# A decoder trunk's hidden steps re-paced: modulation steps at least four granules apart, the second norm's constants behind the output projection, seven fill steps in the norm gap

## The chip, the cores and the metric

One core of a Trainium2 chip runs the whole program. The metric is the device time in microseconds of one execution, lower being better. The kernel before took 2029.11 us in the median of three runs (2023.68 to 2029.93). In the profile PE is the matrix engine (PEld its weight loads), DVE, ACT and POOL are the vector, scalar and general engines, and SP issues most transfers.

## What is computed

One layer of a decoder trunk in float32, for 256 prompt rows and 8 sample rows (264 columns in all, `NT`), width D = 2048. Cut to what matters here:

```python
mod = silu(c) @ w_ada + b_ada                      # 2048 x 12288, nine rows of c
sh1, sc1, gt1, sh2, sc2, gt2 = split(mod, 6)
h = rmsnorm(x, g_pre_mix) * (1 + sc1) + sh1
z = h @ w_in                                       # u, v, q, f, i, ..., three gates
...                                                # branch A: spatial gating
...                                                # branches B, C: gated linear recurrences
merged = sum(sigmoid(gate_n) * (branch_n @ w_branch[n]) for n in range(3))
x = x + gt1 * rmsnorm(merged @ w_out, g_post_mix)
h2 = rmsnorm(x, g_pre_mlp) * (1 + sc2) + sh2
x = x + gt2 * rmsnorm(square(relu(h2 @ w_up)) @ w_down, g_post_mlp)
```

The recurrences also return their final states, and for the eight samples every state (128 x 128 or 128 x 256 a head) is read, updated and written.

## The kernel before

**The large products.** Activations lie transposed, features on partitions, 264 columns wide. Weights stream in as a list of blocks (`Stream`). A block of 512 KB (tile `raw`) is split by ACT (line 111, tile `whi`) and DVE (line 108, tile `wlo`) into a high and a low part, and `granule` issues its 24 matmuls: two output blocks, four blocks of the inner dimension, three products (lines 542 to 544). A granule is the unit in which everything else is paced; 578 are issued, and I count them from the program's start. Blocks are loaded five granules ahead and split two ahead. After each granule `linear` calls `background()`, which counts `now[0]` up by one.

**The hidden work.** Three queues are pumped there. `bg` runs the mixers (transposes, gates, decays, the levels of the recurrence, the outputs), `bs` runs the samples' states, and `ba` runs the modulation: `ada_round(r)` computes one sixth of `mod` in 16 steps. A step is four products with weights of 32 columns and 512 moving columns each (line 290, tile `ada`; eight records in the trace) on two tiles `araw` of 512 KB each. There are two such tiles (`ADA_RAW`), and a step's last statement asks SP for the next two, which can be loaded only once the step's matmuls have read the old ones. SP issues in order, `raw` and `araw` in one line.

**Slots.** A level's matmuls (line 562) and a sample's (line 569) are not issued where they arise but collected in `levels` and `samples` and issued in a `slot()`, at the earliest `AGE` = 2 granules later. A slot opens when the modulation has 0.9 steps owing (0.27 come in per granule), or when something waits and a modulation step may go along (`ba.owed >= 0.0`; a step lowers it by one), or when something has waited three granules. So every level or sample that becomes due while `ba.owed` is not negative takes a modulation step with it, wherever the last one was.

**Samples.** For each of eight samples and each group of heads, `samples_r` has POOL load the state (`st`, line 950) and the value row spread over the partitions (`vbc`, line 955), ACT scales the state (line 975), DVE adds the outer product (line 977), POOL writes it back (line 978), and PE reads it (line 569) into `os`. `finish(i)` is called when a branch needs group i: it drains what is left of the mixer and of the group's samples, and transposes `os` on PE (line 1178).

**Who sets the order.** In the mixer stage PE and POOL keep the order of the program (`manual_schedule`, left at line 1280), while DVE, ACT and SP are ordered by the scheduler of the language. Behind line 1280 the scheduler orders PE as well.

**Behind the mixers.** `ba.drain()` finishes the modulation; `G1`, `A2` and `B2` are made of it; the output projection runs 32 granules (`gated_rows` takes each result), and meanwhile 12 tiles for the last modulation round are loaded into free blocks (`pre`, six steps' worth). Then PE has no projection until the two norms are through: `norms()` (lines 1316, 1318), the residual (line 1342), `norm_rows` (squares on line 211, the samples' sum on line 200, a reciprocal root of eleven small DVE instructions), the scaling (lines 1351, 1352), transposes on PE (line 227), and `modulate` on DVE and ACT (lines 358, 360, then 111 and 108). This is the norm gap. Into it go fill steps of round 5: `fill.pump(5.0)` takes the loading step and four steps, `fill.pump(9.0)` nine more, 13 steps in all. What is left goes on in the MLP at 0.2 a granule, one step in six granules.

Of the kernel before, what the change touches and what calls it, by code (L numbers as in the profile page):

```python
# [11 lines left out]
ALU = mybir.AluOpType  # L12
# [3 lines left out]
P = 128  # L16
D = 2048
KT = D // P
# [3 lines left out]
NC = 1 + NS  # L22
# [23 lines left out]
LOAD_AHEAD = 5  # L46
SPLIT_AHEAD = 2
N_BRANCH = 3
FILL = (5.0, 9.0)
READY = object()  # L50
SLOT_LATE = 0.9
SLOT_WAIT = 3
# [1 line left out]
LEVELS_HELD = 3  # L54
FETCHED = 3
AGE = 2


@with_exitstack
def hybrid_step_kernel(  # L60
# [37 lines left out]
    def const(shape, name, dt=F32):  # L98
        return cp.tile(shape, dt, tag=name, name=name)
# [432 lines left out]
    def granule(w, k0, n, c0, width, accs, xh, xl, k, first, last):  # L532
# [11 lines left out]
                    T.matmul(o, b, xh(k + j), start=False, stop=last and j == n - 1)  # L544
        stream[0].ahead()

    levels, samples = [], []

    def slot():

        lv = [x for x in levels if x[0] + AGE <= now[0]][:2]
        sv = [x for x in samples if x[0] + AGE <= now[0]]
        del levels[:len(lv)]
        del samples[:len(sv)]
        if lv:
            pl = sm([P, 2, 8, 32])
            for i, (_, lhs, rhs, _) in enumerate(lv):
                for h in range(4):
                    for hf in range(2):
                        for b in range(4):  # L560
                            t0 = hf * P + b * 32
                            T.matmul(pl[32 * b:32 * b + 32, i, 2 * h + hf, :], lhs[:, h, t0:t0 + 32], rhs[:, h, t0:t0 + 32], start=True, stop=True)  # L562
        if sv:
            G, qm, os_ = sv[0][1]
            nh = 512 // G.dv
            po = sm([P, G.dv])
            for h in range(4):
                for i, (_, _, b, sts) in enumerate(sv):
                    T.matmul(po[32 * h:32 * h + 32, :], qm[:, h, b, :], sts[h // nh][:, h % nh, :], start=i == 0, stop=i == len(sv) - 1)
        if ba.g and ba.owed >= 0.0:  # L570
            ba.step()
        for i, (_, _, _, put) in enumerate(lv):
            put(pl[:, i])
        if sv:
            if sv[0][2] == 0:
                V.tensor_copy(os_, po)
            else:
                add(os_, os_, po)

    def background():  # L580

        now[0] += 1
        bg.pump(rate[0])
        bs.pump(rate[1])
        ba.owed = min(ba.owed + rate[2], SLOT_LATE) if ba.g else 0.0
        wait = max(now[0] + 1 - AGE - min([x[0] for x in levels + samples] + [now[0]]), 0)
        if ba.owed >= SLOT_LATE or wait and (ba.g and ba.owed >= 0.0 or wait >= SLOT_WAIT):
            slot()

    def new_acc():  # L590
# [2 lines left out]
    def linear(w, k0, nk, c0, width, xh, xl):  # L593

        acc = new_acc()
        kc = min(nk, 1024 // width)
        for kb in range(0, nk, kc):
            granule(w, k0, kc, c0, width, [acc], xh, xl, kb, kb == 0, kb + kc == nk)
            background()
        return acc[:, 0:width // P, 0:NT]  # L600
# [392 lines left out]
    def mixer_r(G):  # L993
# [101 lines left out]
        S.activation(ft.unsqueeze(2), c[:, :, NP - 1:NP], AF.Exp)  # L1095
        yield
        mul(kd, kd, k[:, :, 0:NP])
        yield
        yield READY
        attx = blk([P, 4, P])  # L1100
        ps = sm([P, 4, P])
# [170 lines left out]
    order.__exit__(None, None, None)  # L1272


    ba.drain()
    G1 = const([P, KT, NC], "G1")
    mul(G1, mod[:, 2 * KT:3 * KT, :], gpostT.unsqueeze(2).to_broadcast([P, KT, NC]))
    A2 = const([P, KT, NC], "A2")
    V.scalar_tensor_tensor(A2, mod[:, 4 * KT:5 * KT, :], 1.0, gpre2T.unsqueeze(2).to_broadcast([P, KT, NC]), ALU.add, ALU.mult)
    B2 = mod[:, 3 * KT:4 * KT, :]  # L1280

    x1 = [[blk([P, 1024]) for _ in range(2)] for _ in range(2)]
    for t in range(2):
        for hf in range(2):
# [5 lines left out]
    def gated_rows(m, src, Gv, rows):  # L1290

        k = 2 * m
        sq = tmp([P, 2, NT], "vt")
        S.activation(sq, src, AF.Square)
        g = tmp([P, 2, NP], "gt")
        S.activation(g[:, 0, :], src[:, 0, 0:NP], AF.Copy, scale=Gv[:, k, 0:1])
        V.tensor_scalar(g[:, 1, :], src[:, 1, 0:NP], Gv[:, k + 1, 0:1], None, ALU.mult)
        pt = to_tokens(g)
        mul(gs[:, k:k + 2, :], src[:, :, NP:NT], Gv[:, k:k + 2, 1:NC])
        c0 = (m % 4) * CW  # L1300
        S.copy(rows[0][m // 4][:, c0:c0 + CW].rearrange("p (m f) -> p m f", m=2), pt[:, 0])
# [24 lines left out]
    for m in range(8):  # L1326
        if m in PRE_AT:
            n = N_PRE // len(PRE_AT)
            for k in range(n * PRE_AT.index(m), n * PRE_AT.index(m) + n):
                w = blk([P, 1024])  # L1330
                nc.sync.dma_start(w, w_ada[0, k // 2 * P:(k // 2 + 1) * P, 5 * D + k % 2 * 1024:5 * D + (k % 2 + 1) * 1024])
                pre.append(w)
        gated_rows(m, linear(w_out[0], 0, KT, m * CW, CW, mH, mL), G1, og)
    fill = Queue()
    fill.g.append(ada_round(5, pre))
    r1, r1s = norms()
# [131 lines left out]
```

## Time and profile before

| | |
|---|---|
| median of three runs | 2029.11 us |
| the profiled execution's own time | 2031.4 us |
| its span, first to last instruction | 2029.6 us |
| busy: PE, DVE, ACT, POOL | 1946.7, 1191.6, 998.4, 85.5 us |
| matmuls of the projections, lines 542 to 544 | 3 x 4624 records |
| records of modulation steps, line 290 | 464 (8 a step; some records are missing) |
| granted PE clock, mean | 0.982 |

The span begins at the first instruction and ends at the last. A row of a timeline gives the start, the duration, the engine, the line and operation, the tile written and the tiles read, and in brackets how long the engine had been idle and who released it. Rows of matmuls overlap, so the distance from one start to the next tells what a matmul costs. Times are us from the span's start: the mixers with their recurrences lie between about 404 and 966 us, the third branch until 1088, the output projection until 1215, the norm gap and the first MLP granules until 1276.

### The profile page before, as it was taken

The numbers are of one execution on the slowest core, as the hardware profiler recorded it, in microseconds if no ns is written. First come the engines' busy times: TensorE is split into PE (matmuls) and PEld (weight loads), VectorE is DVE, ScalarE is ACT, GpSimd is POOL, SyncE is SP. The second block draws the span as 40 slices with busy tenths as digits, with TensorE's granted clock in tenths as the row PEclk, the third lists the DMA queues.
The fourth block names the chain that finished last, engine by engine and source line by source line (L and its number), as shares of the span: only waits on it lengthen the run. The fifth ranks groups of instructions, "written<-read, shape, count | busy, mean of one in ns | idle before, by whom it ended". The sixth has DMA issues, their size and how long they took to land.

```text
span 2029.6 us, 42046 instructions
## 1 busy us (share of the span) xinstructions
PE 1946.7 (96%) x16972; PEld 1823.7 (90%) x16972; DVE 1191.6 (59%) x2094; ACT 998.4 (49%) x1773; POOL 85.5 (4%) x128
## 2 busy tenths in 40 slices
PE   6999999989979999999999998999999999999997
PEld 4889999878968888978999994899999999999997
DVE  3566667665656576455655556454555555555565
ACT  5444354655745564544444544455444444454543
POOL 1000000102101001120000000000000000000000
PEclk8999999999989999999999998999999999999998
DMA  9797797778578787788876865655555656556552
GB/s 303 276 344 253 230 304 222 224 224 233 170 227 230 227 239 228 218 256 277 282 247 196 269 199 176 210 183 179 182 182 179 185 178 183 181 180 183 179 177 95
DMA packets 341267, 442.05 MB, mean 218 GB/s; under 512 B 14930, under 2 KB 285008, under 8 KB 341072
## 3 DMA queue, kind: packets, MB, share of 16 engines
q1 hardware_dynamic: 330880, 409.19, 63.5%
q0 software_dynamic: 9120, 28.91, 5.5%
q8 instruction: 133, 2.18, 0.4%
q10 hardware_dynamic: 1072, 1.25, 0.2%
q14 instruction: 62, 0.51, 0.1%
HBM read 427.60 MB, written 11.70 MB: 216 GB/s over the span
## 4 chain that ended last, share of the span: by engine, by line
PE 85%; DMA 9%; DVE 2%; issue 1%; ACT 1%; SPq 0%; POOL 0%; DVEq 0%; ACTq 0%; POOLq 0%
PE mm L542 26%; PE mm L543 25%; PE mm L544 25%; DMA araw<-in_w_ada_dram 4%; PE ada L290 4%; DMA vbc<-vs_d 2%; PE ada L260 1%; DMA b<-in_w_ada_dram 1%; DVE wlo L108 1%; PE sm L703 1%; ACT whi L111 1%; DMA raw<-in_w_in_dram 1%; DMA st<-in_state_gla_dram 0%; DMA b<-in_x_prompt_dram 0%; PE sm L562 0%
## 5 line engine op out<-in xcount | busy, mean ns | idle before, releaser
L542 PE MATMUL mm<-b,whi 128*128 128x264 f32 x4624 | 1328.7, 287 | 7.3 <-DVE b L105 3.4
L543 PE MATMUL mm<-b,whi 128*128 128x264 f32 x4624 | 1320.5, 286 | 0.2 <-DVE b L108 0.2
L544 PE MATMUL mm<-b,wlo 128*128 128x264 f32 x4624 | 1315.8, 285 | 0.3 <-DVE wlo L108 0.2
L108 DVE TENSOR_TENSOR wlo<-raw,whi 128x512 fp32r<-128x512 f32 x1136 | 778.0, 690 | 628.1 <-ACT whi L111 625.7
L111 ACT CAST whi<-raw 128x512 fp32r<-128x512 f32 x1136 | 696.8, 618 | 811.3 <-PE mm L543 719.9
L542 PEld LDWEIGHTS mm<-b,whi 128*128 128x128 f32 x4624 | 873.9, 189 | 65.9 <-issue 29.7
L543 PEld LDWEIGHTS mm<-b,whi 128*128 128x128 f32 x4624 | 873.5, 189 | 5.6 <-issue 5.0
L544 PEld LDWEIGHTS mm<-b,wlo 128*128 128x128 f32 x4624 | 873.5, 189 | 0.7 <-DVE wlo L108 0.7
L105 DVE TENSOR_TENSOR b<-b,mm 128x528 f32<-128x528 f32 x136 | 95.6, 704 | 44.9 <-PE mm L544 44.9
L290 PE MATMUL ada<-araw,cT 128*32 128x512 f32 x464 | 89.3, 650 | 30.7 <-DMA araw<-in_w_ada_dram 30.6
L977 DVE SCALAR_TENSOR_TENSOR st<-vbc,b,st 128x128 f32<-128x128 f32 (+1 forms) x96 | 33.7, 393 | 72.4 <-DMA vbc<-vs_d 71.8
L975 ACT ACTIVATE st<-st,fs 128x128 f32<-128x128 f32 (+1 forms) x96 | 36.5, 429 | 55.6 <-DMA st<-in_state_gla_dram 28.4
L290 PEld LDWEIGHTS ada<-araw,cT 128*32 128x32 f32 x464 | 13.3, 111 | 51.3 <-DMA araw<-in_w_ada_dram 44.0
L260 PE MATMUL ada<-b,cT 128*32 128x256 f32 (+1 forms) x640 | 36.6, 362 | 10.8 <-DMA b<-in_w_ada_dram 10.4
L260 PEld LDWEIGHTS ada<-b,cT 128*32 128x32 f32 x640 | 18.0, 115 | 24.6 <-DMA b<-in_w_ada_dram 8.8
L102 DVE TENSOR_TENSOR b<-b,b 128x512 f32<-128x512 f32 (+1 forms) x47 | 34.2, 744 | 2.5 <-ACT b L1040 1.3
L978 POOL DMA_DIRECT2D out_dram<-st x32 | 23.5, 735 | 136.5 <-DVE st L977 91.0
L108 DVE TENSOR_TENSOR b<-gt,b 128x528 fp32r<-128x528 f32 x32 | 22.7, 708 | 3.3
L955 POOL DMA_DIRECT2D vbc<-vs_d x32 | 24.1, 754 | 1.8 <-DMA vs_d<-sqs 1.3
L111 ACT CAST whi<-araw 128x512 fp32r<-128x512 f32 x20 | 12.4, 621 | 21.6 <-PE mm L543 19.8
L108 DVE TENSOR_TENSOR b<-b 128x1024 f32<-128x1024 f32 (+1 forms) x21 | 22.4, 1069 | 1.0 <-PE sm L562 1.0
L102 DVE TENSOR_TENSOR gt<-vt 128x528 f32<-128x528 f32 x32 | 22.4, 700 | 0.0
(285 smaller groups left out, 812.8 us busy)
## 6 DMA issues: line engine op xcount, KB each, us to landing
raw<-in_w_in_dram SPq DMA_DIRECT2D x232, 512.0 KB, 4.8
raw<-in_w_mlp_up_dram SPq DMA_DIRECT2D x128, 512.0 KB, 3.9
raw<-in_w_mlp_down_dram SPq DMA_DIRECT2D x128, 512.0 KB, 3.6
araw<-in_w_ada_dram SPq DMA_DIRECT2D x116, 512.0 KB, 5.4
b<-in_w_ada_dram SPq DMA_DIRECT2D x60, 512.0 KB, 7.1
raw<-in_w_branch_dram SPq DMA_DIRECT2D x48, 512.0 KB, 4.5
raw<-in_w_out_dram SPq DMA_DIRECT2D x32, 512.0 KB, 3.7
b<-in_w_ada_dram SPq DMA_DIRECT2D x32, 256.0 KB, 6.4
```

Source lines behind the costliest of these rows:

```text
L102: V.tensor_tensor(o, a, b, op=ALU.mult)
L105: V.tensor_tensor(o, a, b, op=ALU.add)
L108: V.tensor_tensor(o, a, b, op=ALU.subtract)
L111: S.copy(hi, src)
L260: T.matmul(acc[32 * j:32 * j + 32, 0:n], cT[:, k, :], w[:, n * j:n * j + n], start=k == 0, stop=k == KT - 1)
L290: T.matmul(acc[32 * j:32 * j + 32, :], cT[:, k, :], ws[j // 2][:, j % 2 * 512:j % 2 * 512 + 512], start=k == 0, stop=k == KT - 1)
L542: T.matmul(o, a, xh(k + j), start=first and j == 0, stop=False)
L543: T.matmul(o, a, xl(k + j), start=False, stop=False)
L544: T.matmul(o, b, xh(k + j), start=False, stop=last and j == n - 1)
L955: nc.gpsimd.dma_start(v, vs_d[G.i, h * nj:h * nj + 4, b, :].partition_broadcast(P))
L975: S.activation(st[:, i, :], st[:, i, :], AF.Copy, scale=fs[:, h0 + i, b:b + 1])
L977: V.scalar_tensor_tensor(st[:, i, :], v[:, i, :], k[:, h0 + i, NP + b:NP + b + 1], st[:, i, :], ALU.mult, ALU.add)
```

## The change

Modulation gets a rule of its own, `ada_due()`: a step is taken only if at least four granules (`ADA_GAP`) have gone by since the last one was taken in a slot. A slot opens when a step is due and owing or something waits, or when something has waited three granules, so levels and samples may now be issued in a slot without a step. `ba.drain()`, `A2` and `B2` move behind the output projection. `FILL` goes from (5, 9) to (4, 4): the loading step and three steps, then four more, seven in all. In `mixer_r` the wait of a mixer ahead of its cross attention is written as two `READY` (each lets a granule go by and costs the queue nothing) in place of a plain `yield` (which costs it one) and one `READY`.

```diff
-FILL = (5.0, 9.0)
+FILL = (4.0, 4.0)
+ADA_GAP = 4
...
+    ada_at = [0]
+    def ada_due():
+        return ba.g and ba.owed >= 0.0 and now[0] >= ada_at[0] + ADA_GAP
...
-        if ba.g and ba.owed >= 0.0:
+        if ada_due():
+            ada_at[0] = now[0]
             ba.step()
...
-        if ba.owed >= SLOT_LATE or wait and (ba.g and ba.owed >= 0.0 or wait >= SLOT_WAIT):
+        if ada_due() and (ba.owed >= SLOT_LATE or wait) or wait >= SLOT_WAIT:
             slot()
...
         mul(kd, kd, k[:, :, 0:NP])
-        yield
+        yield READY
         yield READY
         attx = blk([P, 4, P])
...
-    ba.drain()
     G1 = const([P, KT, NC], "G1")
     mul(G1, mod[:, 2 * KT:3 * KT, :], gpostT.unsqueeze(2).to_broadcast([P, KT, NC]))
-    A2 = const([P, KT, NC], "A2")
-    V.scalar_tensor_tensor(A2, mod[:, 4 * KT:5 * KT, :], 1.0, gpre2T..., ALU.add, ALU.mult)
-    B2 = mod[:, 3 * KT:4 * KT, :]
...
         gated_rows(m, linear(w_out[0], 0, KT, m * CW, CW, mH, mL), G1, og)
+    ba.drain()
+    A2 = const([P, KT, NC], "A2")
+    V.scalar_tensor_tensor(A2, mod[:, 4 * KT:5 * KT, :], 1.0, gpre2T..., ALU.add, ALU.mult)
+    B2 = mod[:, 3 * KT:4 * KT, :]
```

Lines of the changed kernel are one to eight higher than before up to `mixer_r` and its like (290 is 291, 569 is 576, 1103 is 1111).

**The loads of modulation tiles on SP**, in the third recurrence (granules 184 to 200): each `raw` is one granule's block, each pair of `araw` belongs to the step that is taken next. Before:

```order
L283 DMA araw_8956<-in_w_ada_dram 128x1024
L283 DMA araw_8958<-in_w_ada_dram 128x1024
L502 DMA raw_8992<-in_w_in_dram 128x4x256
L502 DMA raw_9027<-in_w_in_dram 128x4x256
L502 DMA raw_9076<-in_w_branch_dram 128x4x256
L502 DMA raw_9114<-in_w_branch_dram 128x4x256
L283 DMA araw_9126<-in_w_ada_dram 128x1024
L283 DMA araw_9128<-in_w_ada_dram 128x1024
L502 DMA raw_9165<-in_w_in_dram 128x4x256
L283 DMA araw_9206<-in_w_ada_dram 128x1024
L283 DMA araw_9208<-in_w_ada_dram 128x1024
```

After:

```order
L284 DMA araw_9178<-in_w_ada_dram 128x1024
L284 DMA araw_9180<-in_w_ada_dram 128x1024
L503 DMA raw_9255<-in_w_in_dram 128x4x256
L503 DMA raw_9293<-in_w_in_dram 128x4x256
L503 DMA raw_9339<-in_w_in_dram 128x4x256
L503 DMA raw_9455<-in_w_branch_dram 128x4x256
L284 DMA araw_9414<-in_w_ada_dram 128x1024
L284 DMA araw_9416<-in_w_ada_dram 128x1024
L503 DMA raw_9496<-in_w_branch_dram 128x4x256
L503 DMA raw_9539<-in_w_in_dram 128x4x256
L503 DMA raw_9573<-in_w_in_dram 128x4x256
L503 DMA raw_9688<-in_w_in_dram 128x4x256
```

Before, the steps here are taken at granules 180, 184, 185, 190 and 192, so that a step follows its predecessor after four, one, five and two granules; now they are taken at 180, 184, 188, 192, 196 and so on. In the whole recurrence stage no step is nearer than four granules to the one before it, where before ten are. The last step of the mixers is taken at granule 284 instead of 272, and nothing is left for the drain behind the output projection.

**The cross attention's operand on DVE**, in the first recurrence (granules 124 to 128). Row L102 (L103) with `b_167` is the product `kd` that PE's lines 1103 (1111) read; `st<-vbc` are sample updates, each waiting for a `vbc` transfer. Before:

```order
L105 TENSOR_TENSOR os_923_5346<-os_923_5346,sm_5961 128x128
L108 TENSOR_TENSOR wlo_5996<-raw_5853,whi_5995 128x512
L977 SCALAR_TENSOR_TENSOR st_5957<-vbc_6069,b_4767,st_5957 128x128 x4
L108 TENSOR_TENSOR wlo_6000<-raw_5853,whi_5999 128x512
L977 SCALAR_TENSOR_TENSOR st_6067<-vbc_6215,b_4767,st_6067 128x128 x3
L102 TENSOR_TENSOR b_6016<-b_6016,b_167 128x512
L977 SCALAR_TENSOR_TENSOR st_6067<-vbc_6215,b_4767,st_6067 128x128
```

After:

```order
L109 TENSOR_TENSOR wlo_5990<-raw_5845,whi_5989 128x512
L103 TENSOR_TENSOR b_6006<-b_6006,b_167 128x512
L109 TENSOR_TENSOR wlo_6047<-raw_5919,whi_6046 128x512
L106 TENSOR_TENSOR os_921_5371<-os_921_5371,sm_6057 128x128
L109 TENSOR_TENSOR wlo_6051<-raw_5919,whi_6050 128x512
L109 TENSOR_TENSOR wlo_6095<-raw_5955,whi_6094 128x512
L985 SCALAR_TENSOR_TENSOR st_5957<-vbc_6106,b_4767,st_5957 128x128 x4
```

The product now stands ahead of the last two sample updates instead of behind one and three quarters of them; the granule at which PE reads it, 126, is the same.

**PE in the norm gap**, among the transposes of the normed rows (`sm`, line 227 or 228) and the modulation steps. Before, the second transposed tile is begun when a step's first half cuts in:

```order
L227 MATMUL sm_15066<-cst,b_15050 128x128
L227 MATMUL sm_15066<-cst,b_15052 128x128
L227 MATMUL sm_15078<-cst,b_15050 128x128
L290 MATMUL ada_14925<-araw_15006,cT 32x512 x2
L227 MATMUL sm_15078<-cst,b_15052 128x128
```

After, three transposed tiles (12 rows) run in a line before the first such row:

```order
L228 MATMUL sm_15035<-cst,b_14995 128x128
L228 MATMUL sm_15035<-cst,b_14997 128x128
L291 MATMUL ada_14918<-araw_15300,cT 32x512
L228 MATMUL sm_15047<-cst,b_14995 128x128
L228 MATMUL sm_15047<-cst,b_14997 128x128
```

Although seven steps are asked for in the gap, the scheduler has put two more and a quarter of a third early, ahead of or among the first projection's matmuls (before, seven steps stand behind the six of `pre`, most of them in halves, the last nearly six granules into the projections). In the MLP there are then a step's rest and six whole steps (granules 339 to 375) instead of two (333 and 339).

**PE at `finish(2)`**, told in words: before, the third group's last sample is read at granule 235 and `os` is transposed at 242; now the last sample's matmuls (line 576) stand at 242 directly ahead of the two transposes (line 1186), since its slot comes later and `finish` drains it.

More of the change, by code (lines that the diff above doesn't have):

```diff
@@ L1272, in hybrid_step_kernel @@
     order.__exit__(None, None, None)
-    ba.drain()
     G1 = const([P, KT, NC], "G1")
     mul(G1, mod[:, 2 * KT:3 * KT, :], gpostT.unsqueeze(2).to_broadcast([P, KT, NC]))
-    A2 = const([P, KT, NC], "A2")
-    V.scalar_tensor_tensor(A2, mod[:, 4 * KT:5 * KT, :], 1.0, gpre2T.unsqueeze(2).to_broadcast([P, KT, NC]), ALU.add, ALU.mult)
-    B2 = mod[:, 3 * KT:4 * KT, :]
     x1 = [[blk([P, 1024]) for _ in range(2)] for _ in range(2)]
@@ L1333, in hybrid_step_kernel @@
         gated_rows(m, linear(w_out[0], 0, KT, m * CW, CW, mH, mL), G1, og)
+    ba.drain()
+    A2 = const([P, KT, NC], "A2")
+    V.scalar_tensor_tensor(A2, mod[:, 4 * KT:5 * KT, :], 1.0, gpre2T.unsqueeze(2).to_broadcast([P, KT, NC]), ALU.add, ALU.mult)
+    B2 = mod[:, 3 * KT:4 * KT, :]
     fill = Queue()
```

## The prediction

> **What bounds the kernel.** I read the page first: its busy times, the chain of work that ended last, the costliest groups.
>
> ```profile
> PE 1946.7 (96%) x16972; PEld 1823.7 (90%) x16972; DVE 1191.6 (59%) x2094; ACT 998.4 (49%) x1773; POOL 85.5 (4%) x128
> PE 85%; DMA 9%; DVE 2%; issue 1%; ACT 1%; SPq 0%; POOL 0%; DVEq 0%; ACTq 0%; POOLq 0%
> 1345.00:2007.00 662.00, 662.00 (x5447) 661.03 (x5446) 385.58 (x590) 317.65 (x527) 0.00 (x0) 1.00 0.58 177
> ```
>
> PE is the bound. The third line, a window deep in the MLP, gives its pace: 662 us over 5447 rows, 0.1215 us a matmul, 2.9 us a granule of 24. The change removes no matmul, so only what stands between them can move: DMA has 9% of the chain. Next the waits of the stretch with the recurrences (404 to 966 us; waited for: total, times, longest), and windows of it and of the quiet stretch behind it (last columns: granted clock, DMA share, GB/s).
>
> ```profile
> PEld ada L290 <- DMA araw<-in_w_ada_dram: 35.1, 17, 7.6
> DVE st L977 <- DMA vbc<-vs_d: 71.8, 19, 6.3
> ACT st L975 <- DMA st<-in_state_gla_dram: 28.4, 12, 5.6
> ACT st L975 <- DMA st<-in_state_hgrn_dram: 27.1, 9, 5.3
> PEld sm L1103 <- DVE b L102: 5.0, 1, 5.0
> PEld sm L562 <- DVE b L102: 3.9, 1, 3.9
> ...
> 404.00:966.00 562.00, 527.34 (x5230) 473.48 (x5223) 332.96 (x622) 303.99 (x613) 68.31 (x95) 0.97 0.76 230
> 966.00:1088.00 122.00, 122.00 (x992) 114.14 (x991) 69.80 (x106) 56.40 (x90) 2.16 (x4) 1.00 0.80 253
> 738.00:751.00 13.00, 10.06 (x111) 5.34 (x111) 11.03 (x16) 5.58 (x11) 0.00 (x0) 0.88 0.95 321
> 905.00:918.00 13.00, 11.02 (x75) 7.62 (x75) 5.98 (x10) 3.45 (x7) 3.61 (x5) 0.87 0.98 312
> ```
>
> PE loses 562.0 - 527.3 = 34.7 us in this stretch, and its largest wait, 35.1 us on the weight-load side, is for modulation tiles. From 966 to 1088 us, where steps are exactly four granules apart, PE is never idle, at a higher DMA share. The same tiles take longer to land in the first stretch:
>
> ```profile
> DMA to landing us min/median/max: 3.6/6.2/13.8
> ...
> DMA to landing us min/median/max: 3.7/4.6/9.6
> ```
>
> (404 to 966, then 966 to 1088 us.) A step one or two granules (3 to 6 us) behind another cannot have its tiles; four granules with what lies between them are over 12 us.
>
> **Steps four apart.** A step that waits, against one that does not:
>
> ```profile
> 428.19 3.23 PE L290 MATMUL ada<-araw,cT 128*32 128x512 f32 x8 [5.45 <-DMA araw<-in_w_ada_dram]
> ...
> 972.54 0.29 PE L544 MATMUL mm<-b,wlo 128*128 128x264 f32 x1
> 972.76 1.06 PE L290 MATMUL ada<-araw,cT 128*32 128x512 f32 x8
> 973.76 0.39 PE L542 MATMUL mm<-b,whi 128*128 128x264 f32 x1
> ```
>
> A free step puts 973.76 - 972.54 = 1.22 us between two matmuls, 1.1 beyond their pace. The 1.2 us is paid for each step in both kernels; a step alone or in a slot with other matmuls costs about the same, so moving them costs nothing in itself. SP's other loads, which queue behind `araw` in its line, are five granules ahead and cover a step that comes later. The waits go, but not wholly: four granules exceed the median landing of 6.2 us and not the longest, 13.8. I leave 6 of the 35.1: **-29** (ends -35 and -17, half of it). After a long wait PE is slow: the step above took 3.23 us for 1.06, and the window's mean clock of 0.97 is 34 us at half clock. Most of these lie in the waits themselves; with fewer waits I take **-3** (0 to -4).
>
> **Operands behind sample updates.** The 5.0 us are one stop of PE's line 1103 for `kd`, which stands on DVE behind two updates that wait for `vbc`; the new order puts it ahead of them: **-5** (0 if an earlier update holds it as long). The 3.9 us are one level whose operand came late; levels now go out in pairs and later, but nothing orders the operand earlier. The second `READY` moves nothing: product and cross attention stand at granules 124 and 126 in both kernels. For the level I take half: **-2** (0 to -3.9). Against this, 71.8 + 28.4 + 27.1 = 127 us of waits for sample transfers sit on DVE and ACT, of which these 8.9 reach PE, 7%. With PE stopping less, more of them may: **+3** (0 to +13, twice as many reaching it).
>
> **The drain at finish(2).** The last sample's matmuls now stand directly ahead of the transposes of `os`, so a chain that was hidden lies on PE's path. Before, at 944 us, it read (DVE, then ACT):
>
> ```profile
> 944.73 0.41 DVE L105 TENSOR_TENSOR os<-os,sm 128x256 f32<-128x256 f32 x1
> 945.72 0.15 DVE L183 TENSOR_SCALAR sx<-sss 128x1 f32<-128x1 f32 x1 [0.58 <-ACT vt L987]
> 948.17 0.16 DVE L189 SCALAR_TENSOR_TENSOR srr<-sa,srr 128x1 f32<-128x1 f32 x1
> ...
> 948.59 0.51 ACT L989 ACTIVATE os<-os,srr 128x256 f32<-128x256 f32 x1
> ```
>
> 949.10 - 944.73 = 4.4 us, and the sample's matmuls ahead of it with no projection to cover their end: **+4.5** (4 to 8, if the update too is late). The other queues do not stand behind it: the next two granules' weights are split already.
>
> **The norm gap.** Two windows of it, then rows of PE, DVE and ACT, the page's row of the weight splits, and two of the late steps:
>
> ```profile
> 1236.10:1242.90 6.80, 6.11 (x19) 2.45 (x20) 1.57 (x3) 1.97 (x4) 0.00 (x0) 0.50 0.40 136
> 1242.90:1263.00 20.10, 20.10 (x135) 14.20 (x134) 13.29 (x34) 11.99 (x21) 0.00 (x0) 1.00 0.70 230
> ...
> 1228.94 1.67 PE L290 MATMUL ada<-araw,cT 128*32 128x512 f32 x2 [4.03 <-DMA araw<-in_w_ada_dram]
> 1230.55 0.60 PE L200 MATMUL sm<-sqs,cst 128*128 128x8 f32 x2
> 1234.41 0.76 PE L227 MATMUL sm<-cst,b 128*128 128x128 f32 x5 [1.52 <-ACT b L1351]
> 1236.79 1.92 PE L290 MATMUL ada<-araw,cT 128*32 128x512 f32 x4 [1.62 <-DMA araw<-in_w_ada_dram]
> 1242.92 0.36 PE L542 MATMUL mm<-b,whi 128*128 128x264 f32 x1
> ...
> 1233.71 0.87 DVE L1352 TENSOR_SCALAR b<-b,rx 128x512 f32<-128x512 f32 x2
> 1235.56 0.17 DVE L102 TENSOR_TENSOR vt<-xsn,A 128x16 f32<-128x16 f32 x1
> 1239.59 0.54 DVE L358 TENSOR_SCALAR vt<-sm,A,mod 128x256 f32<-128x256 f32 x1 [3.65 <-PE sm L227]
> 1240.05 0.70 DVE L108 TENSOR_TENSOR b<-vt,b 128x528 fp32r<-128x528 f32 x1
> ...
> 1235.68 0.57 ACT L360 ACTIVATE vt<-sm,mod,A 128x256 f32<-128x256 f32 x1 [0.71 <-DVE vt L358]
> 1236.28 0.63 ACT L111 CAST b<-vt 128x528 fp32r<-128x528 f32 x1
> ...
> L108 DVE TENSOR_TENSOR wlo<-raw,whi 128x512 fp32r<-128x512 f32 x1136 | 778.0, 690 | 628.1 <-ACT whi L111 625.7
> ...
> 1264.30 1.05 PE L290 MATMUL ada<-araw,cT 128*32 128x512 f32 x4
> 1273.82 1.05 PE L290 MATMUL ada<-araw,cT 128*32 128x512 f32 x4 [1.41 <-DMA araw<-in_w_ada_dram]
> ```
>
> The 4.0 us wait ahead of line 200 stays: the scheduler puts the seventh step's successor at the same place. The second does not: 12 transposes run from 1234.4 to about 1236.3, PE waits to 1236.8 as before, and DVE gets its second tile at once instead of after 3.65 us. The first modulated tile is then ready at about 1237.6: ACT's share ends at 1235.68 + 0.57, its high part 0.63 later, DVE's low part 0.70 after that. With a step's two pieces on PE ahead of it the first projection starts near 1238.0, not 1242.9. From there DVE sets the pace: eight tiles of 0.54 + 0.70 + two small rows (0.35), the second scaling (0.87) and seven weight splits of 0.69 are 18.4 us from 1235.1, and with the last matmuls the fourth granule ends near 1255, where before it ended at 1263: -8. Four halves of steps between 1264 and 1275 go too; a half costs what a whole step does (1.05 us here, 1.06 at 972), so 4 x 1.1 and the wait of 1.4 are -5.8. But 1236.1 to 1242.9 ran at clock 0.50, and the first granule now falls there: 24 x 0.1215 = 2.9 us more, partly under DVE's time, +2.5. Sum **-11** (-14 to -5: the ninth step's tile, asked for only when the eighth's is read, may again stop PE for 4 us with transposes behind it). The moved constants are one DVE row ahead of all this and cost nothing.
>
> [...]
>
> **Steps in the MLP.** What leaves the gap is paid there: seven against two, 5 x 1.2 = **+6**.
>
> **Sum.** -29 - 3 - 5 - 2 + 3 + 4.5 - 11 + 6 = -36.5 us against the profiled execution's 2031.4; its median of three runs is 2.3 lower, so I set 2029.1 - 36.5 = 1992.6, about **1993 us**.
>
> **Rivals.** (a) *The transfers are the bound, and the wait only changes its name.* For it: in the windows at 738 and 905 us the engines were 0.95 and 0.98 busy while PE waited for `araw`. Against it: the whole stretch has 0.76, the quiet one 0.80 without a wait. If it holds, three quarters of the 29 come back as `raw`, `vbc` and `st` waits: 1993 + 22 = 2015, up to 2026. [...] (b) *Slower: sample updates stop DVE's line, and weight splits queue behind them.* Place: the three recurrences, 404 to 966 us, where slots now come later, so POOL refills `st` later. Price: the 127 us; it decides from the point where some 48 of them, 38%, reach PE instead of 7% (the 39.5 us of gain without my allowance, and the 8.9 there are). At half it is 1990 + 64 - 9 = 2045. Against it: splits are two granules (6 us) ahead, and the longest single wait is 6.3. (c) *Nothing at all:* the spacing does not take effect because other waits end last at the same steps; 2029. (d) *More than forecast:* no `araw` wait is left and none replaces it, 1993 - 6 - 3 - 3 - 3 = 1978 or less.
>
> **Chances.** What a measurement can tell from no change here is 0.3%, 6 us. Forecast (1979 to 2012) 0.75; (a) 0.11, nearly all of it below 2023; (b) 0.06; (c) 0.04; (d) 0.04. Faster 0.89, the same 0.05, slower 0.06. The favourable ends sum to the 1978 of (d); of the unfavourable ones (-17, -5 and +13 instead of -29, -11 and +3) not all will come together: two of the three give 2011 to 2015. I take 1978 to 2016.
>
> **What would show it.** Right: in the changed profile's waits of the recurrence stretch, PE's wait for `araw` under 10 us and no stop at line 1111 (the 1103 of before); a stop of about 4.5 us ahead of line 1186; the first projection behind the norms some 23 us after the last output granule, not 28; seven single steps of 1.2 us in the MLP. Wrong: PE idle again by some 30 us there, with `vbc`, `raw` or DVE named, or the first MLP granules still at half clock.

## The result, and the profile after

The changed kernel took **1992.06 us** in the median of four runs (1991.16 to 1995.95), the kernel before, on the same chip, 2028.3 us (2023.68 to 2029.93). The ratio is 0.9829, with a 95% interval of 0.9807 to 0.985. The forecast was 1993 us. The profiled execution took 1991.31 us, its span is 1989.5 us, the mean granted clock 0.986. Line numbers are one higher than before in the first part of the code (step 291, splits 109 and 112, granule 543 to 545) and seven or eight higher in the mixers and behind them.

The page's row of busy times, and the first row of the chain that ended last:

```profile
PE 1927.4 (97%) x16972; PEld 1819.9 (91%) x16972; DVE 1190.4 (60%) x2092; ACT 995.5 (50%) x1773; POOL 86.0 (4%) x128
PE 92%; DMA 4%; DVE 2%; ACT 1%; issue 1%; SPq 0%; POOL 0%; DVEq 0%; ACTq 0%
```

PE was busy for 1946.7 us and is for 1927.4, with the same number of records: the same matmuls, with the waits that count as busy, took 19 us less. DMA had 9% of the chain and has 4%. Now the waits from 404 to 940 us (waited for: total, times, longest), the stretch in which the forecast looked for its proof:

```profile
DVE st L985 <- DMA vbc<-vs_d: 69.1, 20, 5.9
ACT st L983 <- DMA st<-in_state_gla_dram: 40.2, 14, 6.6
ACT st L983 <- DMA st<-in_state_hgrn_dram: 28.8, 9, 5.0
...
PEld ada L291 <- DMA araw<-in_w_ada_dram: 6.6, 4, 1.8
PEld sm L1186 <- ACT os L997: 5.4, 1, 5.4
...
PEld sm L569 <- DVE b L103: 3.9, 1, 3.9
PEld mm L545 <- DVE wlo L109: 3.8, 6, 1.7
PE ada L291 <- DMA araw<-in_w_ada_dram: 3.8, 3, 1.6
```

The wait for modulation tiles fell from 35.1 us to 6.6. There is no row for line 1111 (1103 before). Ahead of line 1186 there is a new stop of 5.4 us. The late level operand (line 569, 562 before) still costs 3.9.

To set the two kernels against each other I cut the span by granules, not by the clock on the wall. Granule 104 begins at 404.6 us before and 404.4 after, granule 242 (the drain at `finish(2)`) at 966.75 and 929.16, granule 290 at 1116.95 and 1084.84. First before, then after:

```profile
404.59:966.75 562.16, 527.50 (x5232) 474.23 (x5229) 332.96 (x621) 304.05 (x614) 68.31 (x95) 0.97 0.76 230
966.75:1116.95 150.20, 150.20 (x1224) 142.34 (x1222) 84.66 (x128) 69.22 (x111) 2.16 (x4) 1.00 0.76 239
```

```profile
404.44:929.16 524.72, 506.47 (x5208) 467.38 (x5205) 332.97 (x622) 302.17 (x615) 68.77 (x95) 0.99 0.81 243
929.16:1084.84 155.68, 155.68 (x1243) 144.88 (x1242) 83.72 (x124) 68.43 (x109) 2.17 (x4) 0.98 0.77 244
```

From granule 104 to 242 the change gains 562.16 - 524.72 = 37.4 us. PE's idle time fell from 34.7 to 18.3 us, its busy time by 21.0: three steps fewer stand there (24 records), and the clock is 0.99 instead of 0.97. From 242 to 290 it gives back 5.5 us: the three steps, and 2.2 us by a slow clock behind the drain. So -32.0 us up to granule 290.

From the last matmul of granule 321 to the first of granule 328, over the norm gap, the time fell from 60.5 to 47.4 us. The seven single steps in the MLP give back 5.9 us (granules 328 to 400). Together -32.0 - 13.1 + 5.9 = -39.2 of the -40.1 us between the two spans; the output projection took the same time within about 0.1 us, and most of the rest lies behind granule 400. The spans of the two profiled executions differ by more than the medians do, 40.1 against 36.2 us.

### The profile page after: what moved, and what is told of

Same layout as the page of the kernel before. It is cut to its first block, busy times and chain, and to the rows that moved or that the text cites. A ratio compares the mean times of both kernels' runs of the same rounds, so it can differ in the third digit from the quotient of the medians.

```text
span 1989.5 us, 42035 instructions
## 1 busy us (share of the span) xinstructions
PE 1927.4 (97%) x16972; PEld 1819.9 (91%) x16972; DVE 1190.4 (60%) x2092; ACT 995.5 (50%) x1773; POOL 86.0 (4%) x128
## 4 chain that ended last, share of the span: by engine, by line
PE 92%; DMA 4%; DVE 2%; ACT 1%; issue 1%; SPq 0%; POOL 0%; DVEq 0%; ACTq 0%
PE mm L543 28%; PE mm L544 27%; PE mm L545 27%; PE ada L291 3%; DMA araw<-in_w_ada_dram 1%; PE ada L261 1%; DMA b<-in_w_ada_dram 1%; PE sm L711 1%; PE sm L569 1%; DMA raw<-in_w_in_dram 1%; DVE wlo L109 1%; PE sm L228 0%; DMA st<-in_state_gla_dram 0%; PE sm L576 0%; PE sm L1087 0%
## 5 line engine op out<-in xcount | busy, mean ns | idle before, releaser
L291 PE MATMUL ada<-araw,cT 128*32 128x512 f32 x464 | 72.9, 621 | 7.5 <-DMA araw<-in_w_ada_dram 7.5
L985 DVE SCALAR_TENSOR_TENSOR st<-vbc,b,st 128x128 f32<-128x128 f32 (+1 forms) x96 | 34.0, 393 | 74.5 <-DMA vbc<-vs_d 69.1
L983 ACT ACTIVATE st<-st,fs 128x128 f32<-128x128 f32 (+1 forms) x96 | 36.9, 430 | 69.0 <-DMA st<-in_state_gla_dram 40.2
L103 DVE TENSOR_TENSOR b<-b,b 128x512 f32<-128x512 f32 (+1 forms) x47 | 34.1, 744 | 1.6 <-ACT b L1048 0.7
L291 PEld LDWEIGHTS ada<-araw,cT 128*32 128x32 f32 x464 | 11.9, 109 | 18.9 <-DMA araw<-in_w_ada_dram 11.5
L112 ACT CAST whi<-araw 128x512 fp32r<-128x512 f32 x20 | 12.4, 621 | 23.0 <-PE mm L544 21.4
L109 DVE TENSOR_TENSOR b<-b 128x1024 f32<-128x1024 f32 (+1 forms) x21 | 22.4, 1068 | 1.4 <-PE sm L569 0.9
L103 DVE TENSOR_TENSOR gt<-vt 128x528 f32<-128x528 f32 x32 | 22.4, 701 | 0.0
```

The source lines that it names most:

```text
L103: V.tensor_tensor(o, a, b, op=ALU.mult)
L109: V.tensor_tensor(o, a, b, op=ALU.subtract)
L112: S.copy(hi, src)
L291: T.matmul(acc[32 * j:32 * j + 32, :], cT[:, k, :], ws[j // 2][:, j % 2 * 512:j % 2 * 512 + 512], start=k == 0, stop=k == KT - 1)
L983: S.activation(st[:, i, :], st[:, i, :], AF.Copy, scale=fs[:, h0 + i, b:b + 1])
L985: V.scalar_tensor_tensor(st[:, i, :], v[:, i, :], k[:, h0 + i, NP + b:NP + b + 1], st[:, i, :], ALU.mult, ALU.add)
```

## The experiments

Three causes were to be told apart: the wait for the step's own tile (my theory), the transfers as a whole (rival (a)), and the order of the other work, which the new slots change too. Then came the terms of the sum that had been guessed: the drain, the gap, the clock. Times below are medians; each ratio is to the kernel before on the same chip, whose medians were 2027.96, 2030.84 and 2031.5 us in the three groups of runs.

| run | us | ratio to before (95%) |
|---|---|---|
| changed kernel | 1992.06 | 0.9829 (0.9807 to 0.985) |
| spacing and late drain, fill (5, 9) | 1999.72 | 0.9855 (0.9832 to 0.9878) |
| fill (4, 4) alone | 2025.12 | 0.9975 (0.9961 to 0.9989) |
| before, steps read a resident tile | 1990.95 | 0.9811 (0.9791 to 0.9831) |
| changed, slots after two granules | 1982.99 | 0.9771 (0.9748 to 0.9793) |
| before, four split buffers | 2065.29 | 1.018 (1.0135 to 1.0225) |
| the same, tiles loaded two steps ahead | 2032.03 | 1.0009 (0.9993 to 1.0025) |
| changed, steps in pairs | 2162.87 | 1.0661 (1.0629 to 1.0692) |
| slots after two, 32 idle matmuls in the gap | 1986.05 | 0.9786 (0.9753 to 0.9818) |
| slots after two, 16 idle matmuls | 1985.25 | 0.9765 (0.9741 to 0.9789) |
| changed, spacing 3 | 2003.78 | 0.9864 (0.9846 to 0.9881) |
| changed, spacing 2 | 2013.73 | 0.992 (0.9896 to 0.9944) |

### The two halves of the change

```diff
 # the changed kernel
-FILL = (4.0, 4.0)
+FILL = (5.0, 9.0)
```

> The changed kernel with the fill counts set back to (5, 9): only the spacing of the steps, the later drain and the second READY are left of the change. My theory: the spacing carries the mixers' part, -32 us at granule 290, and the fill steps the rest, about -13 us in the norm gap against +6 us of single steps behind it; so 1992 + 7 = 1999 us (1995 to 2003), with the first matmul of the up-projection some 2.5 us later than in the changed kernel, and thirteen steps among the first granules again. Rival, that the two parts help each other (fewer transfers in the gap only because the steps before it are spread): 2005 us or more. Rival, that the fill counts bring nothing: 1992 us.

Measured 1999.72 us, -28 us against before where the theory had -29. Its granules from 104 to 290 took 683.8 us, against 712.4 before and 680.4 in the changed kernel; the gap up to granule 328 took 59.7 us, that is, nearly the 60.5 of before. The first projection started 27.2 us after the last output granule, 1.8 later than in the changed kernel (expected 2.5). The spacing carries the mixers' part and next to nothing of the gap.

```diff
 # the kernel before
-FILL = (5.0, 9.0)
+FILL = (4.0, 4.0)
```

> The kernel before with the fill counts (4, 4) alone: the steps stand where they stood ahead of the norm gap. My theory: -13 us in the gap and +6 us of single steps, 2028 - 7 = 2021 us (2017 to 2024), nothing changed up to granule 322. If the gap's gain hangs on the later drain and the later constants, not on the counts: 2028 us.

Measured 2025.12 us. By the ratio that is 5 us less (2 to 8), by the medians of the group 3; I had 7, and the median is 1 us outside my range. Its gap up to granule 328 took 46.9 us, so the gain of the gap comes from the counts and not from the moved drain. Its rows up to granule 290 are those of the kernel before, in the same order on PE, DVE, ACT and POOL, and yet granules 104 to 290 took 719.9 us in this profile and 712.4 in that one: so far apart are two executions of the same work. The two ratios multiply to 0.983, which is that of the whole change: within their intervals the halves add up, and neither is seen to help the other.

### Taking the wait away without spacing

```diff
 # the kernel before
-T.matmul(acc[32 * j:32 * j + 32, :], cT[:, k, :], ws[j // 2][:, j % 2 * 512:j % 2 * 512 + 512], ...)
+T.matmul(acc[32 * j:32 * j + 32, :], cT[:, k, :], cT.rearrange("p k c -> p (k c)"), ...)
```

> The kernel before, with the order of all instructions kept, but the matmuls of the modulation steps read a resident tile instead of the loaded one: all transfers still run, and no step waits for one. (It leaves the modulation weights of three and more of the six parts out of the computation.) My theory, that PE's waits for the step's own tile are what the spacing takes away: the 35 us of them between 404 and 966 us go, with 2 to 4 us of cold clock, and some 6 to 10 us of such waits in the norm gap and ahead of 404 us, so 1980 to 1993 us. Rival, that the transfers as a whole are the limit and the wait only changes its name: PE then waits as long for split weights, sample updates or operands, 2015 us or more. Rival, that the order of the other work (levels in pairs, product ahead of the updates) brought a good part of the 32 us: 2000 to 2015 us.

Measured 1990.95 us, inside my range, but not by my mechanism alone, and I had overlooked a side of the edit. Once no step reads the tiles, nothing holds their loads back. Of `araw`, 58 were issued between 404 and 600 us where before it were 20 (first row before, second this run):

```profile
araw<-in_w_ada_dram SPq DMA_DIRECT2D x20, 512.0 KB, 6.2
```

```profile
araw<-in_w_ada_dram SPq DMA_DIRECT2D x58, 512.0 KB, 6.0
```

And PE then waited for split weights in their place (404 to 940 us; before, the same two rows had 7.6 and 0.7 us):

```profile
PEld mm L542 <- ACT whi L111: 21.9, 19, 2.6
...
PEld mm L544 <- DVE wlo L108: 12.1, 9, 4.5
```

```profile
475.00:490.00 15.00, 9.64 (x77) 8.53 (x76) 6.76 (x16) 7.53 (x16) 3.73 (x5) 0.99 1.03 312
```

In that window of the same run (the last line) the DMA engines were busy throughout (1.03) and PE idled 5.4 of 15 us. Between granules 116 and 144 the run lost 18.8 us against before, and it won 22.4 from there to granule 242. From 104 to 290 it won 12.5 us in all, where my theory had 35 of waits go, and over the norm gap 19.2; so it was luck that the total fell into my range. Rival (a)'s mechanism is real where loads crowd: the wait does change its name. The run can't separate the two causes, so the next one asks for the tile earlier and keeps the loads tied to the steps.

```diff
 # the kernel before
-SPLIT_BUFS = 6
+SPLIT_BUFS = 4
 # and in the second of the two runs also
-ADA_RAW = 2
+ADA_RAW = 4
-        ws = [load(0), load(1)]
+        ws, nxt = [load(0), load(1)], [load(2), load(3)]
-            ws = [load(2 * k + 2), load(2 * k + 3)] if k + 1 < KT else []
+            ws, nxt = nxt, [load(2 * k + 4), load(2 * k + 5)] if k + 2 < KT else []
```

> The kernel before with four buffers for split weights instead of six: a control for the run below, which needs their room. No theory of mine hangs on its time: 2028 us if splits were ready early enough with four, up to 2060 us if each granule now waits a little for its split.

> The control with four buffers for modulation tiles, loaded two steps ahead instead of one; the order of PE's work is that of the kernel before, steps one and two granules apart and all. My theory, that a step waits because its tile is asked for only when the step before has run: the 35 us of such waits between 404 and 966 us fall below 10 us and the time falls by 20 to 35 us against the control, without any spacing. Rival, that the transfers of this stretch are too many for its time however they are asked for: the waits move to the split weights, as they did when the steps read a resident tile, and the time falls by less than 12 us. Rival, that the order of levels and updates brought the gain: within 6 us of the control.

Control 2065.29 us, two ahead 2032.03: -33.3 us, inside the theory's 20 to 35 and far from both rivals, though not all of it where the theory had it. The waits of the weight loads from 404 to 966 us, control first:

```profile
PEld mm L544 <- DVE wlo L108: 26.0, 18, 4.6
PEld ada L290 <- DMA araw<-in_w_ada_dram: 22.0, 13, 3.3
...
PEld mm L542 <- ACT whi L111: 17.5, 20, 2.6
```

```profile
PEld mm L544 <- DVE wlo L108: 30.4, 20, 4.6
...
PEld mm L542 <- ACT whi L111: 19.5, 19, 3.3
```

No row for `araw` is left. The waits for splits took 6.4 us of the 22.0 back, which is what is left of rival (a) here: 3 in 10, not the three quarters that it asked for. By granules, 16.0 us were won between 104 and 290, which is the 22.0 less the 6.4, and 11.6 in the norm gap. In the mixers, with PE's order untouched, the wait goes and the time with it, so the order of levels and updates is not the cause of this wait.

### Putting the wait back

```diff
 # the changed kernel
-ADA_GAP = 4
+ADA_GAP = 8
...
             ba.step()
+            ba.step()
```

> The changed kernel with two steps back to back every eight granules instead of one every four: as many steps, as many bytes, slots as wide apart. My theory: the second step of each of the 20 pairs asks for its tile when the first has run and stops PE for nearly the whole landing, 5 to 7 us (median landing 7.2 us in the changed kernel): 100 to 140 us more, and half clock behind each stop some 10 to 20 us, 2100 to 2150 us. Rival, that the mean number of steps per granule decides and not their distance: 1992 us, within 10 us.

Measured 2162.87 us, 171 more than the changed kernel and above my range. The row of waits over the whole program, for this run and for the changed kernel:

```profile
PEld ada L291 <- DMA araw<-in_w_ada_dram: 174.7, 44, 13.0
```

```profile
PEld ada L291 <- DMA araw<-in_w_ada_dram: 11.5, 6, 4.6
```

The row grew by 174.7 - 11.5 = 163 us, against 171 in the time. I had reckoned 20 pairs at 5 to 7 us. In 19 pairs the second step stops, twice each, once for either of its tiles: 38 of the 44 stops and 164.5 of the 174.7 us, 8.7 a pair. So the number of pairs was right and the price of one too low. Equal numbers of steps and of bytes, and another distance: the distance decides.

```diff
 # the changed kernel
-ADA_GAP = 4
+ADA_GAP = 3   # in the second run 2
```

> The changed kernel with steps at least three granules apart instead of four. My theory, that the landing of a tile (median 7.2 us) against the distance sets the wait: three granules are 8.7 us and the matmuls between, so waits for modulation tiles come up from 6.6 to 8 to 14 us between 404 and 940 us: 1994 to 2000 us, less 2 us where a step no longer meets a slot's stop. Rival, that any rule without adjacent steps does as well: 1992 us, within 2 us.

> The changed kernel with steps at least two granules apart; five of them then stand two and some eight three granules behind another. My theory: two granules are 5.8 us and the matmuls between, at or under the median landing, so waits for modulation tiles of 15 to 28 us between 404 and 940 us against 6.6 with four: 2001 to 2014 us. Rival, that any rule without adjacent steps does as well: 1992 us, within 2 us.

Measured 2003.78 and 2013.73 us. The waits between 404 and 940 us with a distance of three and of two granules:

```profile
PEld ada L291 <- DMA araw<-in_w_ada_dram: 15.0, 11, 4.7
```

```profile
PEld ada L291 <- DMA araw<-in_w_ada_dram: 24.6, 11, 4.9
...
PEld sm L1111 <- DVE b L103: 5.0, 1, 5.0
```

Four granules leave 6.6 us, three 15.0, two 24.6, the free rule of before 35.1: about 9 us of wait a granule, and 10 to 12 us of time (1992, 2004, 2014). Two granules lie inside my range; three took 4 us more than I had expected and waited 1 us longer. With two the stop of 5.0 us for `kd` is there again (line 1111, whose fellow on line 1103 it was before), and the drain's stop on line 1186 is not: these times are not made by the waits for tiles alone.

### The drain, and late operands

```diff
 # the changed kernel
-SLOT_WAIT = 3
+SLOT_WAIT = 2
```

> The changed kernel with a slot opened after two granules of waiting instead of three, so that the last sample's matmuls stand at granule 236 and no longer directly ahead of the transposes of os at 242. My theory: the stop ahead of the transposes (6.0 us, and some 2 us of slow clock behind it) goes, since the chain on DVE and ACT then runs under the projections; more slots cost nothing, as a step alone costs what it costs in a slot: 1992 - 8 = 1984 us (1982 to 1988). Rival, that the chain is late for its operand from the vbc transfer and stops PE wherever it stands: 1990 to 1994 us. Rival, that slots with less in them bring more stops for samples and levels that come out sooner: 1996 us or more.

Measured 1982.99 us, the fastest kernel of this study: 9 us under the changed kernel, and the two ratio intervals don't meet. Why the drain costs more than I had put down shows in the changed kernel's own rows (DVE, ACT, ACT, PE):

```profile
925.09 0.41 DVE L106 TENSOR_TENSOR os<-os,sm 128x256 f32<-128x256 f32 x1
925.54 0.42 ACT L995 ACTIVATE vt<-os 128x256 f32<-128x256 f32 x1 [1.19 <-DVE os L106]
928.26 0.51 ACT L997 ACTIVATE os<-os,srr 128x256 f32<-128x256 f32 x1 [2.22 <-DVE srr L190]
928.82 0.69 PE L1186 MATMUL sm<-cst,os 128*128 128x128 f32 x2 [4.95 <-ACT os L997]
```

PE stands idle for 5 us, and what follows runs at half clock (0.50 from 927.6 to 934.4 us), which costs another 2.2 us. With slots after two granules the scaling of `os` comes well ahead of the transposes, which find it ready:

```profile
908.91 0.51 ACT L997 ACTIVATE os<-os,srr 128x256 f32<-128x256 f32 x1
924.02 0.38 PE L1186 MATMUL sm<-cst,os 128*128 128x128 f32 x2
```

From granule 242 to 290 that run took 153.4 us instead of 155.7. Its waits from 404 to 940 us show that the level operand is no longer late either:

```profile
PEld ada L291 <- DMA araw<-in_w_ada_dram: 3.9, 4, 1.7
...
PEld sm L569 <- DVE b L103: 0.4, 1, 0.4
```

That the levels' stop went as well was not in my theory: with three granules of waiting two levels go out in one slot, and the operand of one was late (3.9 us); with two they go out one by one. Against it stands a new stop of 3.6 us ahead of line 1173, as the third rival had it. The medians show 9 us. That they come from the drain and the levels is likely, since these stops are gone, but the length of the stretch does not show it: in the two runs below whose mixers are the same row by row, granules 104 to 290 took 678.7 and 678.4 us, only 2 less than the changed kernel's 680.4, where this run took 672.5.

### The norm gap and the clock

In the changed kernel PE idles for 3.7 us ahead of a step whose tile is late, and the granted clock is low behind it (rows of PE, then windows of the gap, the clock third from the right):

```profile
1196.64 1.36 PE L291 MATMUL ada<-araw,cT 128*32 128x512 f32 x2 [3.71 <-DMA araw<-in_w_ada_dram]
1197.93 0.60 PE L201 MATMUL sm<-sqs,cst 128*128 128x8 f32 x2
1198.46 1.93 PE L291 MATMUL ada<-araw,cT 128*32 128x512 f32 x6
1201.80 2.82 PE L228 MATMUL sm<-cst,b 128*128 128x128 f32 x12 [1.41 <-ACT b L1358]
1204.55 1.92 PE L291 MATMUL ada<-araw,cT 128*32 128x512 f32 x2
1206.40 1.12 PE L228 MATMUL sm<-cst,b 128*128 128x128 f32 x4
1207.44 1.05 PE L291 MATMUL ada<-araw,cT 128*32 128x512 f32 x2
```

```profile
1197.23:1207.47 10.24, 8.83 (x29) 4.05 (x27) 6.50 (x25) 3.60 (x7) 0.00 (x0) 0.50 0.31 105
1207.47:1210.88 3.41, 3.41 (x17) 1.60 (x17) 0.89 (x4) 0.48 (x1) 0.00 (x0) 1.00 0.38 98
```

Twelve transposes take 2.82 us, and the sum's two matmuls, on which DVE waits, come late. Two runs fill the idle time with matmuls whose result nobody reads.

```diff
 # slots after two granules; behind the new residual x1
+    warm = sm([P, 512])
+    for t in range(2):
+        for hf in range(2):
+            for c in range(2):                       # not in the second run
+                for j in range(4):
+                    T.matmul(warm[32 * j:32 * j + 32, :], cT[:, 0, :], x1[t][hf][:, 512 * c:512 * c + 512], ...)
```

> The changed kernel with slots after two granules, and 32 idle matmuls in the norm gap that read the new residual as its quarters come out of VectorE and write a tile that nobody reads; beside them one fill step moves from the gap to the up-projection (+1.1 us). My theory: the granted clock of 0.5 to 0.69 in the 12 us behind PE's 3.7 us of idling goes to 1.00, the twelve transposes take 1.4 us instead of 2.8, the partition sum comes 0.8 us sooner, and the gap shortens by 2 to 4 us: 1983 - 3 + 1 = 1981 us (1978 to 1984). Rival, that VectorE and ScalarE set the gap and PE's clock is hidden: the transposes are shorter and PE only waits longer ahead of them, 1984 us (1982 to 1987).

> As the run with idle matmuls in the norm gap, with 16 of them instead of 32, so that they end before VectorE's chain does. There 64 rows of them took 7.05 us, and the partition sum behind them came 2.2 us after its operand. My theory: the sum comes with its operand again, the clock stays at 1.00 up to it, and the gap is 23 us or less, against 25.0 with 32 of them and 23.8 with none; one fill step has again moved to the up-projection (+1.1 us): 1982 to 1984 us. Rival, that the clock falls all the same in the second wait of the gap and eats the gain: gap 24 us or more, 1984 to 1987 us.

Measured 1986.05 and 1985.25 us, neither to be told from 1982.99 by its interval, and both in the rival's range and above mine. The profiles say more. From the last output granule to the first projection it was 23.8 us without idle matmuls, 25.0 with 32, 22.5 with 16. With 32 of them:

```profile
1186.54 7.05 PE L1355 MATMUL sm<-b,cT 128*32 128x512 f32 x64
1193.52 0.39 PE L201 MATMUL sm<-sqs,cst 128*128 128x8 f32 x2
1193.84 1.06 PE L291 MATMUL ada<-araw,cT 128*32 128x512 f32 x6
1197.18 1.58 PE L228 MATMUL sm<-cst,b 128*128 128x128 f32 x12 [2.28 <-ACT b L1364]
```

The six matmuls of the step take 1.06 us instead of 1.93 and the transposes 1.58 instead of 2.82: the clock holds until 1198.5 us. But the idle matmuls last past their need, and the sum comes some 2 us behind its operand. With 16 of them:

```profile
1191.78 0.39 PE L201 MATMUL sm<-sqs,cst 128*128 128x8 f32 x2
1194.82 1.05 PE L291 MATMUL ada<-araw,cT 128*32 128x512 f32 x4 [2.65 <-DMA araw<-in_w_ada_dram]
1195.80 2.63 PE L228 MATMUL sm<-cst,b 128*128 128x128 f32 x12
```

The gap is 22.5 us, under the 23 that the theory asked for, but behind the second wait, of 2.65 us, the slow clock is back, as the rival said (0.60 from 1195.8 to 1197.0 us, 0.50 from there to 1199.2), and with the moved step (+1.1) nothing is left that the total shows. The faster clock shortened PE's own rows by 2.1 us (0.87 and 1.24) in the first of these runs, and the gap by 1.4 in the second; but the idle matmuls cost time of their own.

## Why the prediction was right

The total came out as forecast, and the mechanism with it; two terms of the sum were mis-sized, in opposite directions. That it came out to 1 us is luck: these two cancel, and the runs of the kernel before alone lie between 2023.0 and 2035.15 us.

**Steps four apart: the waits.** Forecast -29 with 6 us left; measured -28.5 with 6.6 left. The two-ahead run, the pairs and the distances of three and two show the cause: a tile is asked for when the step before has run, and the distance must cover the landing (3.8 us at the least, 7.2 in the median and 12.4 at the most in the changed kernel, 404 to 940 us).

**The clock of the stretch.** This step failed in size: forecast -3 (0 to -4), "most of these lie in the waits themselves". PE's busy time fell by 21.0 us. Three steps fewer are 3.2 of it. Waits that the weight-load rows show while the matmul row still counts as busy are another 35.1 - 23.6 before and 6.6 - 3.8 after, 8.7 less:

```profile
PE ada L290 <- DMA araw<-in_w_ada_dram: 23.6, 10, 7.5
```

The remaining 9.1 us I put down to the same matmuls at a faster clock. The slow clock does not lie in the waits: of the 34.1 us at half clock between granules 104 and 242 before, PE was busy for 28.6, and now it is for 6.7 of 8.4. Work at half clock took about twice as long (six matmuls of a step 1.93 us in the changed kernel, 1.06 at 1.00 in the run with 32 idle matmuls), so half of the difference of 21.9, 10.9 us, with the waits that count as busy, fits the 9.1. A long wait before, at full clock, and what came behind it:

```profile
423.69:427.10 3.41, 0.00 (x0) 0.00 (x0) 1.03 (x3) 0.00 (x0) 0.00 (x0) 1.00 0.98 309
427.10:433.93 6.83, 5.74 (x19) 2.96 (x20) 0.00 (x0) 0.00 (x0) 0.00 (x0) 0.50 0.80 265
```

That the clock and nothing else makes these 9 us is worked out from the busy times and the granted clock, not tried by itself.

**Operands behind sample updates.** The stop at line 1103 went: -5.0 as forecast. The level operand's 3.9 us stayed, where I had half of it going. The exposed sample waits, +3, fit the one new row that I can put down to them, the late low parts of weights (0.7 before, 3.8 after); but the same mixers with the fill counts alone have 2.3 in this row, so the term is not shown. The waits on DVE and ACT for samples are 69.1 + 40.2 + 28.8 = 138 us, 11 more than before, and still hardly reach PE; rival (b) had its price right and its share wrong.

**The drain at finish(2).** Forecast +4.5 (4 to 8); it is a stop of 5.4 us and 2.2 us by the slow clock, 7.6. My term held the chain and left out what an idle PE costs afterwards, which is the same slip as with the clock above.

With three steps moved out and in again, these make -28.5 - 9.1 - 5.0 + 0 + 3.1 + 7.6 = -31.9 from granule 104 to 290, where -32.0 was measured and -31.5 forecast: 6 us more from the clock against 5 us less from the drain and the levels. That they cancel is luck.

**The norm gap.** Forecast -11, measured -13.1. Inside it the parts differ. The first projection came 2.5 us earlier and not 5, 25.4 us behind the last output granule where the sign was 23. The transposes ran at half clock, 2.82 us where I had 1.9, and behind them stand two halves of a step and four more transposes, 3.9 us up to the projection where I had 1.7. The granules behind it ran faster than I had reckoned: 17.8 us from granule 323 to 328, against 26.4 before.

The +2.5 for a first granule at half clock did not come: the clock was 1.00 again from 1207.5 us on, 0.9 us ahead of the first projection. In neither kernel was the clock 1.00 as soon as matmuls ran: before, from 1236.1 to 1242.9 us, PE was busy for 6.11 of 6.80 us at 0.50, and in the changed kernel the clock stayed at half for 10.2 us, with PE busy for 8.83 of them.

**Steps in the MLP.** Forecast +6, measured +5.9.

**Rival (a)** is not what happened, but its mechanism exists. With the loads let loose PE waited 34 us for split weights where before it were 8, and ACT 63.6 us for `raw` of `w_in` where before it were 13.8. The waits moved within SP's own loads: POOL's `vbc` and the states were waited for no longer than before in that run (62.1 us against 71.8, and 42.4 against 55.5). That a wait moves from SP's loads to POOL's is not shown here.

What stays open: how the 9 us of the slots after two granules divide between drain and levels, and whether they are these alone. Profiled executions of kernels whose mixers are the same row by row took 672.5, 678.7 and 678.4 us for granules 104 to 290, and those with the mixers of before 712.4 and 719.9, so single traces don't settle differences of some 7 us in this stretch. No run tries the two `READY` by themselves; that they have no share is argued in the prediction and not shown.

## What to carry to other kernels

Where a small load is asked for only when its buffer has been read, the distance between two uses must cover the landing, or the load must be asked for two uses ahead (here the waits fell from 35.1 us to 6.6 by the distance, and from 22.0 to none by the earlier load); compare the two times before spreading anything else. Price a stop of the matrix engine with the slow matmuls behind it (here 2.2 us behind one of 5.4), not only with its own length. When work is spread out, look at once for what was hidden behind the clumps: here a drain with nothing left to cover it, a stop of 5 us and a slow clock behind it, which went with one number.

## What the runs showed of the hardware

All of this is read from the profiles of these runs. In the kernel before, between 400 and 1250 us, the granted clock reads 0.50 in stretches that begin at 427.10, 498.78, 584.11, 604.59, 747.95, 778.67, 911.79, 1229.23 and 1236.06 us, and 1.00 in the rest. Each of the nine lasts 3.41 or 6.83 us, and their beginnings lie whole multiples of 3.413 us apart (498.78 - 427.10 = 71.68, 21 times). In the 3.41 us ahead of them PE was busy for 0.00, 0.13, 0.00, 0.47, 1.15, 0.50, 1.43, 0.28 and 1.01 us; within them for 38.1 of 44.4 us. The two windows at 423.69 us above are the first of these: 3.41 us of nothing at 1.00, then 6.83 us at 0.50 with PE at work.

In the changed kernel, in the same part of the span, half clock begins at 582.84, 753.50, 927.58 and 1197.23 us and lasts 3.41, 3.41, 6.83 and 10.24 us. In the 3.41 us ahead PE was busy for 0.96, 2.30, 0.00 and 0.59 us. But from 900.28 to 903.69 us it was busy for 1.95, less than ahead of 753.50, and the clock stayed at 1.00: PE's busy time in the 3.41 us ahead does not settle it alone. In the run with 32 idle matmuls:

```profile
1195.12:1198.53 3.41, 1.35 (x12) 1.29 (x12) 2.94 (x14) 1.41 (x3) 0.00 (x0) 1.00 0.76 231
1198.53:1201.94 3.41, 3.41 (x9) 1.08 (x8) 2.52 (x8) 2.03 (x5) 0.00 (x0) 0.50 0.19 77
1201.94:1205.35 3.41, 3.41 (x18) 1.66 (x17) 0.75 (x4) 0.53 (x1) 0.00 (x0) 1.00 0.43 117
```

PE's stop of 2.28 us leaves it 1.35 us of work in the first window, and the second is at half clock although PE works all through it. So here the work behind a stop of 2.28 us paid for it. No run was built to try how long a stop must be.
